# Layer norm's scale and shift on transposed tiles, with a separate path for the residual rows

## Chip, cores, metric

The kernel runs on one core of a Trainium2 chip. The metric is device time in microseconds (us) of one execution, as the median of several runs.

## What is computed

Two layers of a hybrid decoder trunk on a sequence of 1024 tokens with 1024 channels, all in float32. In each layer a mixer (dilated attention, a gated linear recurrence and a state-space branch behind one input projection, joined by one output projection) and a convolutional feed-forward block are each added to the scaled input and normalized:

```python
def _layer_norm(x, g, b):
    xf = x.astype(jnp.float32)
    mu = jnp.mean(xf, axis=-1, keepdims=True)
    var = jnp.mean(jnp.square(xf - mu), axis=-1, keepdims=True)
    y = (xf - mu) * lax.rsqrt(var + LN_EPS) * g.astype(jnp.float32) + b.astype(jnp.float32)
    return y.astype(x.dtype)
...
    for l in range(DEPTH):
...
        h = _layer_norm(DEEPNORM_ALPHA * h + mix, ln1_g[l], ln1_b[l])
        ffn = _conv_ffn(h, w_up[l], ffn_conv_w[l], ffn_conv_b[l], w_down[l])
        h = _layer_norm(DEEPNORM_ALPHA * h + ffn, ln2_g[l], ln2_b[l])
```

So there are four layer norms. Each output h goes two ways: through the next block's projection, and as the residual (times alpha) into the next sum.

## The kernel before

Rows of h are tokens: eight row tiles of 128 tokens x 1024 channels (NT = 8, `ys[0..7]`). A projection needs h with channels along partitions, so each row tile is transposed on TensorE in blocks of 128x128 (`PE.transpose` with `ident`) into a PSUM bank, from which ScalarE copies it. Float32 matmuls are made of three products of a high and a low part: `split(hi, lo, src)` is a ScalarE copy into the rounded type and a VectorE subtraction for the rest.

`layer_norm` (L1274) takes the statistics of a row tile on VectorE (two `bn_stats`, one `bn_aggr`, then a root on ScalarE and a reciprocal on VectorE). It then applies mean, root, scale and shift in one of two ways, chosen per tile by `LN_ON_V` (L40): two `scalar_tensor_tensor` passes of 128x1024 on VectorE, or one ScalarE activation with scale 1/std and bias -mean/std and then a multiply and an add of 128x1024 on VectorE. Along a row scale and shift vary by column, so `ln_params` (L1268) loads them from DRAM broadcast to all 128 partitions (`lg`, `lb`).

The first norm of a layer (names `y`, `ln1`) stands in `after` (L1749), called for each row tile behind the last group of the output projection (`op03...`, `op13...`). The tile is normalized, stored to the DRAM buffer `hres`, and two tiles later given to `M.put` (L1355): eight transposes into two banks (`ht`), four ScalarE copies into `raw` (`hr`). From `raw` it builds, whenever enough columns are there, the seven moving operands of the up-projection (`B11`, `B21`, `B22`, `T1` to `T4`; in the trace `T0...` and `T1...` with the layer ahead). The up-projection `uP` and the down-projection `dP` use a seven-product scheme on 2x2 blocks, so operands are sums and differences of blocks, made on VectorE.

The up-projection goes over 24 pairs of column tiles (`pairs`, L1545). Each pair loads two weight tiles (`wu`), prepares seven weight operands (`wA`, `wS`), issues 84 matmuls, and applies the convolution and the gate (`cg`, `cv`); the product is stored to DRAM (`gd`). Before the down-projection the eight row tiles are loaded back from `hres` as `yf` and scaled by alpha on ScalarE (L1570 to L1574); the down-projection's results are added onto them by VectorE. In layer 0 the second norm (`ln20`, through `lagged`, L1309) stores each tile to `hres` and `to_hT` (L1295) transposes it, with hi taken by ScalarE from PSUM and lo by VectorE from PSUM, for layer 1's input projection (`ups1`, `vps_1`, `q1`, `k1`). Layer 1 loads the rows from `hres` again later as `y` and scales them by alpha (L1732, L1733). The last norm (`ln21`) goes to the output.

Nothing is issued in the order in which it is written. All calls are recorded, and a planner (`Graph`, `make_plan`) gives every call an order and every tile a place: it sweeps the calls forwards and backwards several times with estimated durations, limits how early an instruction may stand before it is due (`AHEAD`), and respects the number of buffers (46 slots of 128x1024, `NSLOT`; 8 half slots; 8 PSUM banks). Each engine then runs its own list strictly in that order; all DMAs are issued from SP's queue. All instructions are issued from one helper, so the trace gives line L146 for all of them, and tiles are told apart by their names.

Of the kernel before, what the change touches and what calls it, by code (L numbers as in the profile page):

```python
# [21 lines left out]
NT = 8  # L22
# [17 lines left out]
LN_ON_V = {"10": (0, 2, 4, 6, 7), "11": (0, 2, 4, 6, 7), "20": (1, 3, 5, 7), "21": (0, 2, 4, 6, 7)}  # L40
# [11 lines left out]
def layout(x, w_in, lru_conv_w, lru_conv_b, lru_wr, lru_br, lru_wi, lru_bi, lru_lambda, s5_a_re, s5_a_im, s5_b_re,  # L52
# [15 lines left out]
    def state4(a):  # L68
# [13 lines left out]
        "fcw": ffn_conv_w.reshape(L, 3, 48, 128).transpose(3, 0, 2, 1), "fcb": chan(ffn_conv_b, 48),  # L82
        "bglu": chan(s5_b_glu, 2), "are": state(s5_a_re), "aim": state(s5_a_im),
# [413 lines left out]
def emit(tc, A, out, planner, trace):  # L497
    nc = tc.nc
    V, ACT, POOL, PE, SP = (Traced(e, planner.calls) for e in (nc.vector, nc.scalar, nc.gpsimd, nc.tensor, nc.sync))
    with ExitStack() as ctx:  # L500
# [48 lines left out]
        def load_w(src, name):  # L549
# [4 lines left out]
            return hi, lo  # L554

# [718 lines left out]
        def layer_norm(i, y, gb, name, by_half=False):  # L1274
# [6 lines left out]
            if by_half:  # L1281
                (a, b), (ga, gg), (ba, bb) = (halves(t) for t in (y, *gb))
                for x, gx, bx in ((a, ga, ba), (b, gg, bb)):
                    stt(x, x, mv[:, 0:1], gx, ALU.subtract, ALU.mult)
                    stt(x, x, mv[:, 2:3], bx, ALU.mult, ALU.add)
            elif i in (LN_ON_V[name[2:4]]):
                stt(y, y, mv[:, 0:1], gb[0], ALU.subtract, ALU.mult)
                stt(y, y, mv[:, 2:3], gb[1], ALU.mult, ALU.add)
            else:
                stt(mv[:, 3:4], mv[:, 0:1], -1.0, mv[:, 2:3], ALU.mult, ALU.mult)  # L1290
                ACT.activation(y, y, AF.Identity, scale=mv[:, 2:3], bias=mv[:, 3:4])
                mul(y, y, gb[0])
                add(y, y, gb[1])

        def to_hT(i, y, name):  # L1295
            if i % 4 == 0:
                hT_tiles(name, i // 4)
            c = slice(i % 4 * 128, i % 4 * 128 + 128)
            for h in range(2):
                ps = bank(f"{name}h{h}")  # L1300
                for k in range(4):
                    PE.transpose(ps[:, k * 128:(k + 1) * 128], y[:, (4 * h + k) * 128:(4 * h + k + 1) * 128], ident)
                for q in range(2):
# [38 lines left out]
        class Moving:  # L1342
# [12 lines left out]
            def put(self, i, y):  # L1355
# [4 lines left out]
                d = slice(i % 4 * 128, i % 4 * 128 + 128)  # L1360
                for h in range(2):
                    ps = bank(f"ht{l}{i}{h}")
                    for k in range(4):
                        PE.transpose(ps[:, k * 128:(k + 1) * 128], y[:, (4 * h + k) * 128:(4 * h + k + 1) * 128], ident)
                    for q in range(2):
                        ACT.activation(t_slice(self.raw[2 * h + q, c], d),
# [419 lines left out]
```

## Time and profile before

| | us |
|---|---|
| median of 3 runs (lowest, highest) | 2337.41 (2333.17, 2340.06) |
| the profiled execution | 2334.8 |
| its span, first to last instruction | 2333.0 |
| TensorE (PE) busy in the span | 2263.2 (97%) |
| VectorE (DVE) busy | 2051.2 (88%) |
| ScalarE (ACT) busy | 1136.1 (49%) |
| DMA, share of 16 engines | 28.0% |

Busy time is the part of the span in which an engine runs an instruction. The granted clock is that of TensorE as a share of full speed. Instructions that follow each other directly on VectorE overlap a little, so from start to start they take less than their busy time.

### The profile page before, as it was taken

The page shows a single profiled execution, that of the slowest core. Times are in us where ns is not written, and L with a number is a line of the kernel's source. Part 1 is how long each engine was busy: PE and PEld are TensorE (multiplying, and loading weights), DVE is VectorE, ACT ScalarE, POOL GpSimd, SP SyncE. Part 2 cuts the span into 40 slices and gives each one's busy share as a digit, 9 for nine tenths or more (in the row PEclk, how much of TensorE's full clock was granted, in tenths as well). Part 3 has the DMA queues.
Part 4 walks back from the last instruction along what each step waited for, and adds up shares of the span by engine and source line. Part 5 has one row for each costly group of instructions (what it writes and reads, how often), then busy time and mean ns, then how long its engine had stood idle before and what let it go on. Part 6 is the DMA issues. An engine that isn't in the chain of part 4 may idle for free.

```text
span 2333.0 us, 28165 instructions
## 1 busy us (share of the span) xinstructions
PE 2263.2 (97%) x10520; PEld 1818.2 (78%) x10520; DVE 2051.2 (88%) x3362; ACT 1136.1 (49%) x1766; POOL 4.0 (0%) x8
## 2 busy tenths in 40 slices
PE   7999999999999999999899999999999999999996
PEld 6877778778888888888678677787888888878885
DVE  8797788998888889999995877789879899899999
ACT  4265673454444446444433646825345454464442
POOL 0000000000000000000000000000000000000000
PEclk9999999989999999999999999999999999999998
DMA  5321141212223226222333211412122232262312
GB/s 195 85 79 44 46 149 55 82 63 94 78 73 101 83 96 225 100 99 100 110 98 92 64 53 42 149 50 100 37 82 82 90 100 99 83 240 80 133 70 90
DMA packets 75257, 221.18 MB, mean 95 GB/s; under 512 B 11696, under 2 KB 20016, under 8 KB 75120
## 3 DMA queue, kind: packets, MB, share of 16 engines
q1 hardware_dynamic: 75120, 219.38, 28.0%
q8 instruction: 82, 1.34, 0.2%
q14 instruction: 55, 0.45, 0.1%
HBM read 163.65 MB, written 48.23 MB: 91 GB/s over the span
## 4 chain that ended last, share of the span: by engine, by line
PE 83%; DVE 13%; ACT 1%; DMA 1%; issue 1%; DVEq 0%; ACTq 0%; SPq 0%
PE uP_n L146 35%; PE dP_n L146 14%; PE o_n L146 3%; DVE yf_n L146 3%; PE s_n L146 2%; PE pt_n L146 2%; PE yps_n L146 1%; DVE daP_n L146 1%; DVE dbP_n L146 1%; DVE cg_n L146 1%; DVE gr_n L146 1%; DMA wu_n<-in_w_up_dram 1%; DVE wr_n L146 1%; DVE cv_n L146 1%; PE ups00c_n L146 1%
## 5 line engine op out<-in xcount | busy, mean ns | idle before, releaser
L146 PE MATMUL dP_n<-dbP_n,daP_n 128*128 128x512 f32 x2016 | 463.3, 392 | 18.3 <-DVE yf_n L146 17.7
L146 PEld LDWEIGHTS dP_n<-dbP_n,daP_n 128*128 128x128 f32 x2016 | 380.5, 189 | 98.9 <-issue 9.5
L146 ACT ACTIVATE dbP_n<-wr_n 128x512 fp32r<-128x512 f32 x168 | 102.0, 627 | 128.8 <-DVE wr_n L146 65.2
L146 DVE SCALAR_TENSOR_TENSOR cg_n<-ga_n,small,cg_n 128x1023 f32<-128x1023 f32 x96 | 122.7, 1280 | 26.6 <-ACT cg_n L146 26.1
L146 ACT ACTIVATE wS_n<-wu_n 128x512 fp32r<-128x512 f32 x144 | 89.9, 629 | 114.9 <-PE uP_n L146 66.7
L146 ACT ACTIVATE wA_n<-wu_n 128x512 fp32r<-128x512 f32 x144 | 88.9, 626 | 95.3 <-PE uP_n L146 47.7
L146 DVE TENSOR_TENSOR yf_n<-yf_n,dP_n 128x512 f32<-128x512 f32 x192 | 127.7, 689 | 3.7 <-PE dP_n L146 2.9
L146 ACT ACTIVATE daP_n<-gr_n 128x512 fp32r<-128x512 f32 x144 | 87.7, 626 | 86.3 <-PE dP_n L146 48.4
L146 DVE SCALAR_TENSOR_TENSOR cv_n<-va_n,small,cv_n 128x1023 f32<-128x1023 f32 x96 | 122.9, 1281 | 6.1 <-ACT cv_n L146 5.3
L146 DVE TENSOR_TENSOR dbP_n<-wr_n,dbP_n 128x512 fp32r<-128x512 f32 x168 | 116.1, 694 | 1.0 <-ACT dbP_n L146 1.0
L146 DVE TENSOR_TENSOR wS_n<-wu_n,wS_n 128x512 fp32r<-128x512 f32 x144 | 98.0, 688 | 15.2 <-ACT wS_n L146 14.8
L146 DVE TENSOR_TENSOR wA_n<-wu_n,wA_n 128x512 fp32r<-128x512 f32 x144 | 97.8, 687 | 7.2 <-ACT wA_n L146 6.9
L146 DVE TENSOR_TENSOR daP_n<-gr_n,daP_n 128x512 fp32r<-128x512 f32 x144 | 99.1, 693 | 1.3 <-ACT daP_n L146 1.2
L146 DVE CUSTOM_DVE_ANT_0 P_n<-s_n,mask_n 128x512 f32<-128x512 f32 (+3 forms) x96 | 55.3, 587 | 45.6 <-PE s_n L146 37.7
L146 ACT ACTIVATE cg_n<-ga_n,small 128x1024 f32<-128x1024 f32 x48 | 59.5, 1242 | 50.8 <-DVE ga_n L146 42.2
L146 ACT ACTIVATE cv_n<-va_n,small 128x1024 f32<-128x1024 f32 x48 | 59.7, 1243 | 42.6 <-DVE va_n L146 26.7
L146 PE MATMUL o_n<-PT_n,vt_n 128*64 128x256 f32 (+1 forms) x480 | 80.2, 380 | 0.0
L146 DVE TENSOR_TENSOR uu_n<-uP_n,p_n 128x512 f32<-128x512 f32 x96 | 65.6, 687 | 14.2 <-PE uP_n L146 14.1
L146 PE MATMUL pt_n<-ident,P_n 128*128 128x128 f32 x432 | 73.7, 281 | 1.2 <-ACT k11r_n L146 0.8
L146 PEld LDWEIGHTS pt_n<-ident,P_n 128*128 128x128 f32 x432 | 50.7, 141 | 28.2 <-issue 16.6
L146 PE MATMUL uP_n<-T0T2h_n,wS_n 128*128 128x512 f32 x192 | 65.3, 401 | 4.1 <-DVE wS_n L146 3.6
L146 PE MATMUL uP_n<-T1T1h_n,wS_n 128*128 128x512 f32 x192 | 63.7, 392 | 3.6 <-ACT T1T1h_n L146 3.6
(2300 smaller groups left out, 5973.7 us busy)
## 6 DMA issues: line engine op xcount, KB each, us to landing
wu_n<-in_w_up_dram SPq DMA_DIRECT2D x96, 512.0 KB, 3.5
gd<-cg_n SPq DMA_DIRECT2D x48, 512.0 KB, 2.8
gr_n<-gd SPq DMA_DIRECT2D x48, 512.0 KB, 4.7
wr_n<-in_w_down_dram SPq DMA_DIRECT2D x48, 512.0 KB, 4.4
hres<-y_n SPq DMA_DIRECT2D x16, 512.0 KB, 2.6
yf_n<-hres SPq DMA_DIRECT2D x16, 512.0 KB, 5.1
xT_n<-in_xT_dram SPq DMA_DIRECT2D x16, 256.0 KB, 5.9
y_n<-in_x_dram SPq DMA_DIRECT2D x8, 512.0 KB, 4.0
```

What stands on the lines that cost most here:

```text
L146: i = f(*args, **kwargs)
```

## The change

Scale and shift leave the row tiles. A row tile is only normalized, always by ScalarE, and stored to `hres` that way. Tiles are transposed two by two: four banks, each with two channel blocks of two tiles; `turned` applies scale and shift while ScalarE evacuates a bank, where they are one number per partition, read from the table of small parameters (`small`, which gets four more entries). `put` and `to_hT` use it; in `to_hT` the evacuation goes to a half slot, and hi and lo are split from there. The residual path applies scale and shift (both multiplied by alpha beforehand) to the rows in a block of its own: it loads a row tile from `hres`, multiplies, adds, and stores it back. For a layer's first norm that block lies in the pairs 12 to 19 of its up-projection (`RES`), one tile to a pair; for the second norm of layer 0 ahead of the second group of attention heads of layer 1 (`RESP`). The scaling by alpha where the rows are loaded is dropped, except for the input x. The last norm is applied by VectorE for all tiles.

```diff
-LN_ON_V = {"10": (0, 2, 4, 6, 7), "11": (0, 2, 4, 6, 7), "20": (1, 3, 5, 7), "21": (0, 2, 4, 6, 7)}
+RES = 12
+RESP = 1
...
+        def normalize(y, name):
+
+            mv = moments(y, name)
+            stt(mv[:, 3:4], mv[:, 0:1], -1.0, mv[:, 2:3], ALU.mult, ALU.mult)
+            ACT.activation(y, y, AF.Identity, scale=mv[:, 2:3], bias=mv[:, 3:4])
+
+        def turned(l, which, ys, i, name, into):
+
+            g, b = par(f"l{which}g", l), par(f"l{which}b", l)
+            for q in range(4):
+                ps = bank(f"{name}{q}")
+                for k in range(2):
+                    for t in range(2):
+                        PE.transpose(ps[:, (2 * k + t) * 128:(2 * k + t + 1) * 128],
+                                     ys[i + t][:, (2 * q + k) * 128:(2 * q + k + 1) * 128], ident)
+                o = into(q)
+                for k in range(2):
+                    ACT.activation(o[:, k, :], ps[:, k * 256:k * 256 + 256], AF.Identity,
+                                   scale=g[:, 2 * q + k:2 * q + k + 1], bias=b[:, 2 * q + k:2 * q + k + 1])
+                yield q, o
+
+        def residual(l, which):
+
+            gb = ln_params(l, which)
+            for t in gb:
+                ACT.activation(t, t, AF.Identity, scale=ALPHA)
+
+            def apply(y):
                 mul(y, y, gb[0])
                 add(y, y, gb[1])
 
-        def to_hT(i, y, name):
+            return apply
...
+        def to_hT(l, ys, i, name):
             if i % 4 == 0:
                 hT_tiles(name, i // 4)
-            c = slice(i % 4 * 128, i % 4 * 128 + 128)
...
-                    ACT.activation(hi, pv, AF.Identity)
-                    sub(lo, pv, hi)
...
+            c = slice(i % 4 * 128, i % 4 * 128 + 256)
+            for q, o in turned(l, 1, ys, i, name, lambda q: two_k(half(f"{name}o{q}"))):
+                split(*(two_k(t)[:, :, c] for t in hT[q, i // 4]), o)
...
-            def put(self, i, y):
+            def put(self, i, ys):
...
+                d = slice(i % 4 * 128, i % 4 * 128 + 256)
+                for _ in turned(l, 0, ys, i, f"ht{l}{i}", lambda q: t_slice(self.raw[q, c], d)):
+                    pass
...
             for n, u in enumerate(pairs[:-2]):
+                if n == RES:
+                    apply = residual(l, 0)
+                if RES <= n < RES + NT:
+                    y = slot(f"yr{l}{n - RES}")
+                    SP.dma_start(out=y, in_=rows(n - RES))
+                    apply(y)
+                    SP.dma_start(out=rows(n - RES), in_=y)
...
-                SP.dma_start(out=y, in_=hres[i * 128:(i + 1) * 128, :])
-                ACT.activation(y, y, AF.Identity, scale=ALPHA)
+                SP.dma_start(out=y, in_=rows(i))
...
+                if l and p == RESP:
+                    apply = residual(l - 1, 1)
+                    for i in range(NT):
+                        y = slot(f"yr{l}{i}")
+                        SP.dma_start(out=y, in_=rows(i))
+                        apply(y)
+                        SP.dma_start(out=rows(i), in_=y)
...
             def after(i):
-                layer_norm(i, ys[i], gb, f"ln1{l}{i}")
-                SP.dma_start(out=hres[i * 128:(i + 1) * 128, :], in_=ys[i])
-                if i >= 2:
-                    M.put(i - 2, ys[i - 2])
+                normalize(ys[i], f"ln1{l}{i}")
+                SP.dma_start(out=rows(i), in_=ys[i])
+                if i in (3, 5, 7):
+                    M.put(i - 3, ys)
...
                 if n == 0:
-                    M.put(6, ys[6])
-                if n == 1:
-                    M.put(7, ys[7])
+                    M.put(6, ys)
```

## Rows read from the trace of the kernel before

**Rows 1.** The page: span, busy time by engine, chain that ended last by engine.
```profile
span 2333.0 us, 28165 instructions
PE 2263.2 (97%) x10520; PEld 1818.2 (78%) x10520; DVE 2051.2 (88%) x3362; ACT 1136.1 (49%) x1766; POOL 4.0 (0%) x8
...
PE 83%; DVE 13%; ACT 1%; DMA 1%; issue 1%; DVEq 0%; ACTq 0%; SPq 0%
```

**Rows 2.** Table by stage: stretch and length, busy us by engine, granted clock, DMA.
```profile
440.00:500.00 60.00, 52.66 (x224) 40.85 (x223) 59.21 (x87) 38.24 (x68) 0.00 (x0) 0.89 0.19 64
...
550.00:890.00 340.00, 340.00 (x1500) 281.31 (x1499) 285.59 (x376) 153.67 (x211) 1.91 (x2) 1.00 0.26 87
890.00:1100.00 210.00, 209.94 (x926) 173.51 (x926) 207.31 (x333) 106.07 (x172) 0.00 (x0) 1.00 0.39 138
1100.00:1200.00 100.00, 86.16 (x403) 70.56 (x402) 99.64 (x184) 41.49 (x80) 0.00 (x0) 0.93 0.32 107
...
1310.00:1590.00 280.00, 280.00 (x1404) 213.51 (x1403) 221.54 (x379) 150.56 (x236) 0.00 (x0) 1.00 0.21 68
1590.00:1660.00 70.00, 64.17 (x293) 49.81 (x292) 68.38 (x107) 39.07 (x81) 0.00 (x0) 0.93 0.24 86
...
1700.00:2050.00 350.00, 349.81 (x1538) 288.19 (x1537) 309.44 (x404) 168.12 (x228) 0.00 (x0) 1.00 0.29 96
```

**Rows 3.** TensorE's waits: for whom, us in total, times, longest.
```profile
PE dP_n L146 <- DVE yf_n L146: 17.7, 4, 8.4
...
PE uP_n L146 <- ACT T1T1h_n L146: 3.6, 1, 3.6
```

**Rows 4.** Timeline of VectorE, 425 to 500 us: start, busy us, instruction.
```profile
424.32 1.22 DVE L146 TENSOR_TENSOR y_n<-y_n,lb_n 128x1024 f32<-128x1024 f32 x1
425.46 1.28 DVE L146 SCALAR_TENSOR_TENSOR y_n<-y_n,mv__ln,lb_n 128x1024 f32<-128x1024 f32 x1
...
456.61 1.28 DVE L146 SCALAR_TENSOR_TENSOR y_n<-y_n,mv__ln,lb_n 128x1024 f32<-128x1024 f32 x1
...
477.95 1.23 DVE L146 TENSOR_TENSOR T0T4l_n<-hr_n,T0T4h_n 128x1024 fp32r<-128x1024 f32 x1
```

**Rows 5.** Timeline of TensorE, same stretch; in brackets idle before and releaser.
```profile
466.32 0.72 PE L146 MATMUL uP_n<-T0T1h_n,wS_n 128*128 128x512 f32 x1 [2.16 <-ACT T0T1h_n L146]
468.07 0.79 PE L146 MATMUL uP_n<-T0T1l_n,wS_n 128*128 128x512 f32 x1 [1.02 <-DVE T0T1l_n L146]
469.33 0.79 PE L146 MATMUL uP_n<-T0T2h_n,wS_n 128*128 128x512 f32 x1 [0.47 <-ACT T0T2h_n L146]
...
475.22 1.22 PE L146 MATMUL uP_n<-T0T2h_n,wS_n 128*128 128x512 f32 x2 [3.65 <-DVE wS_n L146]
```

**Rows 6.** Timeline of VectorE, then of TensorE, 1100 to 1182 us.
```profile
1128.37 1.28 DVE L146 SCALAR_TENSOR_TENSOR yf_n<-yf_n,mv__ln,lg_n 128x1024 f32<-128x1024 f32 x1
...
1174.59 1.29 DVE L146 SCALAR_TENSOR_TENSOR yf_n<-yf_n,mv__ln,lb_n 128x1024 f32<-128x1024 f32 x1
...
1149.53 7.09 PE L146 MATMUL dP_n<-dbP_n,daP_n 128*128 128x512 f32 x24 [8.41 <-DVE yf_n L146]
```

**Rows 7.** Timeline of VectorE, 1590 to 1660 us.
```profile
1595.44 1.27 DVE L146 SCALAR_TENSOR_TENSOR y_n<-y_n,mv__ln,lg_n 128x1024 f32<-128x1024 f32 x1
...
1619.37 1.28 DVE L146 SCALAR_TENSOR_TENSOR y_n<-y_n,mv__ln,lb_n 128x1024 f32<-128x1024 f32 x1
```

**Rows 8.** ScalarE's groups by tile and shape: count, busy us, mean ns, idle before.
```profile
L146 ACT ACTIVATE y_n<-y_n 128x1024 f32<-128x1024 f32 x16 | 16.8, 1053 | 10.3 <-DMA y_n<-hres 5.0 <-PE o_n L146 3.2 <-DMA y_n<-in_x_dram 2.0
L146 ACT ACTIVATE y_n<-y_n,mv__ln 128x1024 f32<-128x1024 f32 x6 | 7.6, 1263 | 2.2 <-DVE mv__ln L146 2.2
```

**Rows 9.** Weight split's group on ScalarE; DMA issues: count, KB, us to landing.
```profile
L146 ACT ACTIVATE wA_n<-wu_n 128x512 fp32r<-128x512 f32 x144 | 88.9, 626 | 95.3 <-PE uP_n L146 47.7 <-DMA wu_n<-in_w_up_dram 14.0 <-DVE cv_n L146 7.7
...
wu_n<-in_w_up_dram SPq DMA_DIRECT2D x96, 512.0 KB, 3.5
gd<-cg_n SPq DMA_DIRECT2D x48, 512.0 KB, 2.8
```

More of the change, by code (lines that the diff above doesn't have):

```diff
@@ L554, in load_w, with rows @@
             return hi, lo
+        def rows(i):
+            return hres[i * 128:(i + 1) * 128, :]
         def half(name):
@@ L1280, in layer_norm @@
             rstd(mv[:, 2:3], mv[:, 1:2], 1, 1)
[L1281 to L1291, printed above, removed]
+            return mv
@@ new lines, in layer_norm @@
+        def layer_norm(y, gb, name, by_half=False):
+            mv = moments(y, name)
+            for a, ga, ba in zip(*(halves(t) for t in (y, *gb))) if by_half else ((y, *gb),):
+                stt(a, a, mv[:, 0:1], ga, ALU.subtract, ALU.mult)
+                stt(a, a, mv[:, 2:3], ba, ALU.mult, ALU.add)
+        def normalize(y, name):
+            mv = moments(y, name)
+            stt(mv[:, 3:4], mv[:, 0:1], -1.0, mv[:, 2:3], ALU.mult, ALU.mult)
+            ACT.activation(y, y, AF.Identity, scale=mv[:, 2:3], bias=mv[:, 3:4])
@@ L1359, in put @@
                         self.raw[q, c] = slot(f"hr{l}{q}{c}")
[L1360 to L1366, printed above, removed]
-                                       ps[:, q * 256:q * 256 + 256].rearrange("p (k c) -> p k c", k=2), AF.Identity)
-                if i == 3:
+                d = slice(i % 4 * 128, i % 4 * 128 + 256)
+                for _ in turned(l, 0, ys, i, f"ht{l}{i}", lambda q: t_slice(self.raw[q, c], d)):
+                    pass
+                if i == 2:
                     for name, q0 in (("B11", 0), ("B21", 2)):
@@ L1597, in store @@
                         def store(i):
-                            SP.dma_start(out=hres[i * 128:(i + 1) * 128, :], in_=ys[i])
-                        after, tail = lagged(ys, gb, f"ln2{l}", store)
+                            SP.dma_start(out=rows(i), in_=ys[i])
+                        after, tail = lagged(l, ys, f"ln2{l}", store)
                 def product(p, ops, i):
@@ L1731, in emit @@
                 y = slot(f"y{l}{i}")
-                SP.dma_start(out=y, in_=(A["x"] if l == 0 else hres)[i * 128:(i + 1) * 128, :])
-                ACT.activation(y, y, AF.Identity, scale=ALPHA)
+                SP.dma_start(out=y, in_=A["x"][i * 128:(i + 1) * 128, :] if l == 0 else rows(i))
+                if l == 0:
+                    ACT.activation(y, y, AF.Identity, scale=ALPHA)
                 ys.append(y)
@@ L1749, in after @@
             def after(i):
-                layer_norm(i, ys[i], gb, f"ln1{l}{i}")
-                SP.dma_start(out=hres[i * 128:(i + 1) * 128, :], in_=ys[i])
-                if i >= 2:
-                    M.put(i - 2, ys[i - 2])
+                normalize(ys[i], f"ln1{l}{i}")
+                SP.dma_start(out=rows(i), in_=ys[i])
+                if i in (3, 5, 7):
+                    M.put(i - 3, ys)
             out_group(l, sp, 3, rl, ys, after)
```

40 lines of the change are left out of this document (17 added, 23 removed).

## The prediction

> **What bounds the kernel now.** I read the page first. TensorE is busy for 97% of the span and the chain that ended last lies on it for 83%, with 13% on VectorE [rows 1]. So little is to be had outside the 69.8 us in which TensorE is idle (2333.0 less 2263.2), and what VectorE costs matters only where TensorE waits for it. Next I read the table by stage, to see where those 69.8 us lie [rows 2]. Three stretches are the seams where a layer norm stands between two matmul stages: 440 to 500 us (first norm of layer 0, seam A) has 7.34 us idle, 1100 to 1200 (second norm of layer 0, seam B) 13.84, 1590 to 1660 (first norm of layer 1, seam C) 5.83. That is 27.0 us. In each VectorE is busy nearly throughout (59.21 of 60, 99.64 of 100, 68.38 of 70). Elsewhere TensorE is full: 340.00 of 340, 280.00 of 280, 349.81 of 350 us. The list of TensorE's waits says the same from the other side: what it waits for is a tile that VectorE, or ScalarE right behind VectorE, writes last [rows 3].
>
> The same table holds a second loss. The mean granted clock of the seams is 0.89, 0.93 and 0.93, and 1.00 elsewhere [rows 2]. Two levels occur, 2.4 and 1.2 GHz, so 13.2, 14.0 and 9.8 us were spent at the lower one (for A 60 x 0.11 / 0.5). In A the fall comes with the gaps that end at 466.32 and 475.22 us [rows 5]. A part of the slow time is idle and already counted; of what is busy, half is lost. In A the gaps of 1.02, 0.47 and 3.65 us lie in it [rows 5], so about 8 us are busy and 4 are lost; for B I take 3 and for C 3.4. Together the seams cost 11.3 + 16.8 + 9.2 = 37.3 us. No gain can be much more.
>
> **What leaves VectorE at the seams.** Each norm today ends in two passes of 128x1024 on VectorE, either two scalar_tensor_tensor (1.28 us busy each) or, behind ScalarE's normalization, a multiply and an add (1.22 each, the next one starting 1.14 us on) [rows 4]. Afterwards there is none: ScalarE does (y - mean) x rstd for every tile, and scale and shift ride on the evacuation of the transposes, where they lie along partitions. What counts is what leaves the stretch in which VectorE is saturated. In A, 12 such passes lie from 424.32 to 456.61, and VectorE then works without a break until the last operand of the up-projection at 477.95 [rows 4]. At about 1.17 us from start to start these are 14.0 us, against 11.3 of loss. In B there are 16 passes between 1128.37 and 1174.59, 18.7 us against 16.8, and the largest gap, 8.41 us, ends at 1149.53 with seven of the 16 before it [rows 6]. In C there are ten from 1595.44 to 1619.37, 11.7 us against 9.2 [rows 7]. So in each seam the credit just exceeds the loss.
>
> **What joins the seams.** ScalarE gets the normalization of the tiles that had none: five tiles more in A and in C, four more in B, at 1.263 us each [rows 8]. Every evacuation now takes a scale and a bias per partition. Nearest row: the same Identity on 128x1024 takes 1.263 us with both and 1.053 without [rows 8], so 0.21 us more on each of 32 evacuations, 6.7 us a seam. In B each operand of the next layer also passes one more ScalarE copy (16 of 128x512, 0.63 us each by the weight split's row [rows 9]). ScalarE's sum goes from 38.2 to about 51 of 60 us in A and from 41.5 to about 63 of 100 in B [rows 2]: no bound, but a hop on the chain of the last pair. Transposes are as many as before; tiles go two by two, so an even tile waits for its odd neighbour, which the operands built from column pairs did before too. I take back 1 us in A, 2.5 in B (eight evacuations 0.21 longer, and the copy) and 1.5 in C, where the margin is thinnest. The reach of these terms is 0 to half of each seam's loss. What is left to gain is 10.3 + 14.3 + 7.7 = 32.3 us.
>
> One rule of the Trainium skill speaks against the move: its page "ScalarE: Activation LUTs", section "Rules for kernel authors", says that adds and multiplies belong on VectorE and not on ScalarE. The rows show for this type and size 1.22 us a pass on VectorE and 1.263 for scale and shift together on ScalarE [rows 4, 8], so here the trace does not bear it out; by the rule, ScalarE would be the later engine and rival 3 would hold.
>
> **What moves into other stages.** The residual needs the scaled rows too. A block per row tile loads it, multiplies, adds and stores it again: 8 tiles, three times. Two of these blocks lie in pairs 12 to 19 of the up-projections, one tile to a pair, the third ahead of the second attention group of layer 1. Each tile is two VectorE passes, 2.3 us from start to start; 18.4 us a block, 55 us in all, which roughly equals what the seams lose. The cover: in 550 to 890 us TensorE issues 1500 matmuls in 340 us, so a pair of 84 lasts 19.0 us; VectorE is busy for 285.59 of 340, which leaves 3.0 us a pair. In layer 1 it is 309.44 of 350, or 2.2 us a pair for 2.3 of work [rows 2]: just full. That VectorE is full need not stop TensorE: from 890 to 1100 us VectorE is busy for 207.31 of 210 and TensorE for 209.94 [rows 2]. The attention stage has 58 us free [rows 2]. Bounds: 0 (all covered, or a little below, since VectorE's busy time shrinks when instructions stand back to back) to 18.4 us for each block. I take 1.5 for each of the two in the up-projections, nearest to the row of 890 to 1100, and nothing in attention.
>
> Each tile also adds a load and a store on SP's queue (48 of 512 KB in all; the loads of scales and shifts stay eight, six of them now ahead of a block instead of a seam). SP waits before each store until VectorE has added; the next weight load stands behind it. The store of each pair's gated product (gd) waits for VectorE in the same way 48 times already, and it takes no TensorE time. A weight load lands 3.5 us after its issue [rows 9]. ScalarE loses 24 scalings by alpha (1.05 us each by their twin's row [rows 8]) and gains six on the parameters: nothing, as it has room.
>
> The order of all instructions is written by a planner that starts anew with other calls. Stages that are gapless now may get small gaps, or lose the few they have. Bounds: -3 to +10 us; I take 3.
>
> **Sum.** The profiled execution took 2334.8 us, 1.8 around its span. 2334.8 - 32.3 + 3 + 3 = 2308.5. The median of the runs is 2.6 us above the profiled one, so I forecast 2311 us, a gain of 1.1%.
>
> **Rivals.** Rival 1, slower: room in SBUF. The seven operands of the up-projection hold 28 of 46 slots (7 names, 2 halves, hi and lo); 18 are left for a pair's 14 tiles and the loads of the next. The residual holds two parameters and one or two row tiles through eight pairs a layer. If the next pair's weights then come only when a slot falls free, TensorE waits up to the 3.5 us of landing in each of 16 pairs: 56 us. 2311 + 56 - 3 = 2364; from 2.4 us a pair it is slower than before by over 0.3%. Against it: no weight load is among TensorE's waits [rows 3], and ScalarE waits for them 14.0 us over 144 copies [rows 9]. The skill's page "Trainium Kernel Development and Optimization", section "Best Practices", says that regular bubbles can mean that SBUF ran out; the trace has none there. Rival 2, no change: the planner pushes the residual towards the down-projection, where VectorE is full, or up-projection and attention take most of it: 30 to 40 of the 55 us show, 2311 + 32 - 3 = 2340, from about 2330. Rival 3, a half gain: ScalarE's longer evacuations become the last link at the seams. 2311 + 16 = 2327.
>
> **How the numbers follow.** Forecast (2297 to 2320) 0.64; rival 3 and smaller leaks (2320 to 2330) 0.17; rival 2 0.09; rival 1 0.10. Of 2337, 0.3% is 7 us, about the least that a measurement of this kernel tells from no change. Faster by more: 0.64 + 0.17 = 0.81; within: 0.09; slower: 0.10. The range takes in the ceiling, 2337.4 - 37.3 less a few us by which a new order may be luckier, and reaches up into rival 2: 2297 to 2335.
>
> **What would show it.** Right: in the stretches of the three seams TensorE's idle falls from 27 us to under 8 and the granted clock to 0.97 or more; VectorE's sum over the span stays within 10 us; the waits for yf in seam B are gone; the up-projections hold over 99% on TensorE with VectorE some 18 us busier. Wrong: TensorE waits for weight loads in pairs 12 to 19 (rival 1), VectorE multiplies and adds of rows after the down-projection has begun (rival 2), gaps at the seams that end on ScalarE's evacuations (rival 3).

## Result and profile after

| | us |
|---|---|
| before, median of 4 runs (lowest, highest) | 2336.65 (2333.17, 2340.06) |
| after, median of 4 runs (lowest, highest) | 2303.27 (2301.57, 2303.53) |
| ratio, with its 95% interval | 0.9856 [0.9839, 0.9873] |
| profiled execution of after, its span | 2303.5, 2301.7 |

The kernel became 1.4% faster; the forecast was 2311 us, 1.1%. The page of after answers to [rows 1]: span, busy time by engine, the chain that ended last by engine, then the new DMA issues (count, KB, us to landing). Instructions that stood at L146 before stand at L149 now.

```profile
span 2301.7 us, 28256 instructions
...
PE 2242.8 (97%) x10520; PEld 1811.4 (79%) x10520; DVE 2045.1 (89%) x3357; ACT 1154.0 (50%) x1773; POOL 4.0 (0%) x8
...
PE 84%; DVE 10%; ACT 3%; DMA 2%; issue 1%; DVEq 0%; ACTq 0%; SPq 0%
...
yr_n<-hres SPq DMA_DIRECT2D x24, 512.0 KB, 3.8
hres<-yr_n SPq DMA_DIRECT2D x24, 512.0 KB, 3.2
```

VectorE's sum hardly moved (2051.2 to 2045.1 us) while its share of the chain fell from 13% to 10%: the passes were not saved, they were moved to where TensorE doesn't wait for them.

Since the two orders differ, equal clock times don't hold equal work. From here on the span is cut at five matmuls that every version has: the first of the last group of layer 0's output projection (`op03`), the last of its up-projection (`uP`), the last of the first product of layer 1's input projection (`ups1`), and for layer 1 again the first of the last output group (`op13`) and the last of the up-projection. This gives six stages: mixer of layer 0 (all up to that last output group); A (last output group, first norm, up-projection); B (down-projection, second norm, first product of layer 1); mixer of layer 1 (the rest of the input projection, attention, the other output groups); C, as A for layer 1; the end. The table by stage, first of before, then of after; columns: stretch and length, busy us (and count) of PE, PEld, DVE, ACT, POOL, granted clock, DMA share, GB/s.

```profile
0.00:406.90 406.90, 391.05 (x1996) 302.80 (x1997) 334.06 (x739) 216.32 (x336) 2.04 (x6) 0.99 0.30 94
406.90:918.50 511.60, 503.91 (x2226) 413.58 (x2225) 451.34 (x618) 240.84 (x357) 1.91 (x2) 0.99 0.28 94
918.50:1194.60 276.10, 262.26 (x1172) 216.19 (x1172) 273.12 (x466) 127.20 (x224) 0.00 (x0) 0.98 0.32 114
1194.60:1569.80 375.20, 370.34 (x1900) 283.00 (x1899) 291.34 (x518) 200.61 (x310) 0.00 (x0) 0.99 0.25 75
1569.80:2081.00 511.20, 504.10 (x2226) 412.31 (x2225) 456.25 (x623) 244.41 (x362) 0.00 (x0) 0.99 0.28 96
2081.00:2333.00 252.00, 231.54 (x1009) 190.35 (x1007) 245.11 (x403) 106.72 (x180) 0.00 (x0) 0.97 0.28 103
```

```profile
0.00:397.50 397.50, 383.68 (x1992) 298.71 (x1993) 331.52 (x739) 214.71 (x336) 2.04 (x6) 0.99 0.31 95
397.50:901.10 503.60, 500.71 (x2230) 411.83 (x2229) 451.03 (x622) 254.86 (x366) 1.92 (x2) 1.00 0.32 111
901.10:1163.20 262.10, 260.19 (x1181) 214.35 (x1180) 258.43 (x442) 138.02 (x233) 0.00 (x0) 1.00 0.34 119
1163.20:1544.50 381.30, 365.45 (x1882) 283.27 (x1881) 305.14 (x535) 192.78 (x303) 0.00 (x0) 0.97 0.31 99
1544.50:2048.60 504.10, 501.64 (x2234) 412.65 (x2233) 453.31 (x624) 256.58 (x370) 0.00 (x0) 1.00 0.31 108
2048.60:2301.70 253.10, 231.09 (x1008) 190.61 (x1006) 245.69 (x400) 97.04 (x167) 0.00 (x0) 0.96 0.33 117
```

The stages that hold the seams became 8.0, 14.0 and 7.1 us shorter, 29.1 together; TensorE's idle time in them fell from 28.6 us (7.7 + 13.8 + 7.1) to 7.3 (2.9 + 1.9 + 2.5), and the granted clock rose from 0.99, 0.98 and 0.99 to 1.00. Two other stages moved that no step of the sum had priced: the mixer of layer 0, which the change does not touch, is 9.4 shorter, and the mixer of layer 1 is 6.1 longer, with 15.9 us idle and a clock of 0.97. The end is 1.1 longer. In all -31.3 us.

TensorE's waits in after, answering to [rows 3]: for whom, us in total, times, longest.

```profile
PE dP_n L149 <- DVE yf_n L149: 11.8, 2, 10.9
PE pt_n L149 <- DVE P_n L149: 10.1, 5, 4.9
...
PE uP_n L149 <- DVE uu_n L149: 5.0, 7, 2.0
```

The wait of 10.9 us for yf stands at the end of the kernel; of those in seam B, 8.41 the longest before [rows 6], one of 0.8 us is left. New is the second line: attention's transposes wait for the probabilities `P`. ScalarE's groups (count, busy us, mean ns, idle before): the evacuations of before, then evacuations and normalizations of after, answering to [rows 8]:

```profile
L146 ACT ACTIVATE hr_n<-ht_n 128x256 f32<-128x256 f32 x64 | 21.4, 389 | 11.8 <-PE ht_n L146 11.5
...
L149 ACT ACTIVATE hr_n<-ht_n,small 128x256 f32<-128x256 f32 x64 | 32.7, 574 | 6.0 <-PE ht_n L149 5.9
...
L149 ACT ACTIVATE y_n<-y_n,mv__ln 128x1024 f32<-128x1024 f32 x16 | 20.0, 1250 | 3.8 <-DVE mv__ln L149 3.8
```

VectorE's last operand of the first up-projection, answering to the last line of [rows 4], and the table for the stretch from the start of A to the end of that operand, first of before, then of after:

```profile
461.98 1.22 DVE L149 TENSOR_TENSOR T0T4l_n<-hr_n,T0T4h_n 128x1024 fp32r<-128x1024 f32 x1
```

```profile
406.90:479.20 72.30, 64.95 (x296) 51.31 (x295) 69.63 (x108) 35.32 (x74) 0.00 (x0) 0.91 0.20 75
...
397.50:463.20 65.70, 64.34 (x313) 52.64 (x311) 56.96 (x102) 47.41 (x83) 0.00 (x0) 1.00 0.21 81
```

### The profile page after: what moved, and what is told of

It is laid out like the page before. It is cut to its first block, busy times and chain, and to the rows that moved or that the text cites. A ratio compares the mean times of both kernels' runs of the same rounds, so it can differ in the third digit from the quotient of the medians.

```text
span 2301.7 us, 28256 instructions
## 1 busy us (share of the span) xinstructions
PE 2242.8 (97%) x10520; PEld 1811.4 (79%) x10520; DVE 2045.1 (89%) x3357; ACT 1154.0 (50%) x1773; POOL 4.0 (0%) x8
## 4 chain that ended last, share of the span: by engine, by line
PE 84%; DVE 10%; ACT 3%; DMA 2%; issue 1%; DVEq 0%; ACTq 0%; SPq 0%
PE uP_n L149 34%; PE dP_n L149 17%; PE o_n L149 3%; PE s_n L149 2%; PE pt_n L149 2%; DVE yf_n L149 1%; PE yps_n L149 1%; DVE cg_n L149 1%; DMA wu_n<-in_w_up_dram 1%; DVE daP_n L149 1%; PE ups00c_n L149 1%; DVE dbP_n L149 1%; PE gtps01c_n L149 1%; PE vps_01c_n L149 1%; DVE cv_n L149 1%
## 5 line engine op out<-in xcount | busy, mean ns | idle before, releaser
L149 PE MATMUL dP_n<-dbP_n,daP_n 128*128 128x512 f32 x2016 | 462.2, 391 | 12.6 <-DVE yf_n L149 11.8
L149 PEld LDWEIGHTS dP_n<-dbP_n,daP_n 128*128 128x128 f32 x2016 | 379.6, 189 | 92.5 <-issue 12.5
L149 ACT ACTIVATE dbP_n<-wr_n 128x512 fp32r<-128x512 f32 x168 | 102.8, 627 | 104.7 <-DVE wr_n L149 49.7
L149 ACT ACTIVATE wA_n<-wu_n 128x512 fp32r<-128x512 f32 x144 | 89.9, 628 | 122.4 <-PE uP_n L149 41.9
L149 ACT ACTIVATE wS_n<-wu_n 128x512 fp32r<-128x512 f32 x144 | 90.2, 630 | 111.5 <-DVE wu_n L149 41.3
L149 ACT ACTIVATE daP_n<-gr_n 128x512 fp32r<-128x512 f32 x144 | 89.5, 628 | 112.8 <-PE dP_n L149 48.2
L149 DVE SCALAR_TENSOR_TENSOR cg_n<-ga_n,small,cg_n 128x1023 f32<-128x1023 f32 x96 | 122.9, 1280 | 23.4 <-ACT cg_n L149 22.6
L149 DVE SCALAR_TENSOR_TENSOR cv_n<-va_n,small,cv_n 128x1023 f32<-128x1023 f32 x96 | 122.8, 1280 | 16.2 <-ACT cv_n L149 16.0
L149 DVE TENSOR_TENSOR yf_n<-yf_n,dP_n 128x512 f32<-128x512 f32 x192 | 127.9, 689 | 4.4 <-PE dP_n L149 2.4
L149 DVE TENSOR_TENSOR dbP_n<-wr_n,dbP_n 128x512 fp32r<-128x512 f32 x168 | 116.0, 694 | 0.3 <-ACT dbP_n L149 0.3
L149 DVE TENSOR_TENSOR daP_n<-gr_n,daP_n 128x512 fp32r<-128x512 f32 x144 | 99.8, 694 | 2.4 <-ACT daP_n L149 2.4
L149 DVE TENSOR_TENSOR wS_n<-wu_n,wS_n 128x512 fp32r<-128x512 f32 x144 | 98.2, 687 | 3.3 <-ACT wS_n L149 2.8
L149 DVE TENSOR_TENSOR wA_n<-wu_n,wA_n 128x512 fp32r<-128x512 f32 x144 | 97.8, 687 | 3.1 <-ACT wA_n L149 2.9
L149 ACT ACTIVATE cg_n<-ga_n,small 128x1024 f32<-128x1024 f32 x48 | 59.7, 1243 | 73.9 <-DVE ga_n L149 51.2
L149 PE MATMUL pt_n<-ident,P_n 128*128 128x128 f32 x432 | 74.3, 285 | 11.2 <-DVE P_n L149 10.1
L149 PEld LDWEIGHTS pt_n<-ident,P_n 128*128 128x128 f32 x432 | 53.4, 144 | 33.7 <-DVE P_n L149 11.6
L149 DVE CUSTOM_DVE_ANT_0 P_n<-s_n,mask_n 128x512 f32<-128x512 f32 (+3 forms) x96 | 55.4, 586 | 22.6 <-PE s_n L149 21.9
L149 ACT ACTIVATE cv_n<-va_n,small 128x1024 f32<-128x1024 f32 x48 | 59.4, 1238 | 24.7 <-DVE va_n L149 18.5
L149 PE MATMUL o_n<-PT_n,vt_n 128*64 128x256 f32 (+1 forms) x480 | 71.1, 375 | 0.0
L149 DVE TENSOR_TENSOR uu_n<-uP_n,p_n 128x512 f32<-128x512 f32 x96 | 65.9, 687 | 3.7 <-PE uP_n L149 3.4
L149 PE MATMUL uP_n<-T1T4h_n,wA_n 128*128 128x512 f32 x192 | 64.0, 394 | 2.1 <-DVE uu_n L149 2.1
L149 PE MATMUL uP_n<-T0T3h_n,wS_n 128*128 128x512 f32 x192 | 63.4, 391 | 2.3 <-DVE uu_n L149 2.3
## 6 DMA issues: line engine op xcount, KB each, us to landing
wu_n<-in_w_up_dram SPq DMA_DIRECT2D x96, 512.0 KB, 3.5
gd<-cg_n SPq DMA_DIRECT2D x48, 512.0 KB, 2.9
gr_n<-gd SPq DMA_DIRECT2D x48, 512.0 KB, 4.4
wr_n<-in_w_down_dram SPq DMA_DIRECT2D x48, 512.0 KB, 5.1
yr_n<-hres SPq DMA_DIRECT2D x24, 512.0 KB, 3.8
hres<-yr_n SPq DMA_DIRECT2D x24, 512.0 KB, 3.2
hres<-y_n SPq DMA_DIRECT2D x16, 512.0 KB, 2.6
yf_n<-hres SPq DMA_DIRECT2D x16, 512.0 KB, 5.2
```

The source lines that it names most:

```text
L149: i = f(*args, **kwargs)
```

## Experiments

Stage lengths in us of the profiled executions, in brackets TensorE's idle time, and the median of the runs with its ratio to before (timed anew beside each):

| version | mixer 0 | A | B | mixer 1 | C | median, ratio |
|---|---|---|---|---|---|---|
| before | 406.9 | 511.6 (7.7) | 276.1 (13.8) | 375.2 (4.9) | 511.2 (7.1) | 2336.65 |
| after | 397.5 | 503.6 (2.9) | 262.1 (1.9) | 381.3 (15.9) | 504.1 (2.5) | 2303.27, 0.9856 |
| first norms only | 400.6 | 501.5 (0.5) | 279.9 (14.3) | 362.2 (2.2) | 505.2 (3.3) | 2304.22, 0.9854 [0.9839, 0.9869] |
| second norm only | 404.0 | 520.7 (16.3) | 264.3 (4.1) | 381.3 (10.3) | 513.3 (8.7) | 2337.13, 1.0003 [0.9993, 1.0012] |
| no residual blocks | 398.7 | 505.1 (2.5) | 262.9 (2.3) | 355.0 (0.0) | 501.9 (1.2) | 2280.42, 0.9754 [0.9740, 0.9769] |
| later block | 399.7 | 508.0 (5.7) | 263.0 (2.7) | 362.3 (2.3) | 502.8 (2.6) | 2290.44, 0.9800 [0.9785, 0.9815] |
| passes back | 415.9 | 516.8 (8.9) | 278.0 (11.4) | 373.9 (7.1) | 512.8 (9.5) | 2349.55, 1.0044 [1.0027, 1.0060] |
| before, other order 1 | 426.0 | 512.5 (8.9) | 285.6 (20.3) | 362.8 (1.2) | 512.0 (8.9) | 2347.02, 1.0035 [1.0019, 1.0051] |
| before, other order 2 | 413.8 | 512.9 (9.1) | 277.4 (14.6) | 367.3 (4.5) | 511.0 (7.4) | 2337.78, 0.9998 [0.9988, 1.0009] |
| after, other order 1 | 407.2 | 504.9 (3.9) | 260.7 (2.0) | 374.1 (12.5) | 501.8 (0.4) | 2305.31, 0.9875 [0.9853, 0.9897] |
| after, other order 2 | 404.3 | 504.1 (3.4) | 261.3 (1.5) | 383.6 (12.5) | 502.0 (1.3) | 2307.91, 0.9881 [0.9865, 0.9897] |
| later block, other order 1 | 413.8 | 504.5 (4.1) | 261.1 (1.2) | 368.2 (0.0) | 500.6 (1.1) | 2292.95, 0.9813 [0.9794, 0.9831] |
| residual on GpSimd | 401.1 | 544.0 (29.3) | 262.3 (3.1) | 376.6 (8.8) | 532.7 (26.0) | 2374.33, 1.0152 [1.0137, 1.0167] |
| residual in place | 397.5 | 505.1 (4.1) | 260.6 (1.7) | 363.8 (0.3) | 502.1 (2.1) | 2281.86, 0.9768 [0.9753, 0.9784] |

**One norm at a time.** Layer 0's second norm goes back to the passes on VectorE and to transposes tile by tile, and its residual block goes:

```diff
-                normalize(ys[i], f"{name}{i}")
+                old_norm(i, ys[i], gb, f"{name}{i}")
...
-                if l and p == RESP:
-                    apply = residual(l - 1, 1)
...
```

> Only the first norm of each layer is changed (seams A and C, and the residual block in pairs 12 to 19); the second norm of layer 0 stays as before, with scale and shift on the rows. Theory (the seams pay, each by the VectorE passes that leave it): from the start of the last output group to the end of the up-projection layer 0 gets 8 us shorter and layer 1 7 us, seam B keeps its 14 us of idle, and outside nothing moves by plan but a few us either way by the new order: 15 us less than before, 2321 (2313 to 2329). Rival (the gain is mostly a lucky order of the whole program): the gain does not follow the seams; seam B shrinks as well, or A and C do not.

And the other way round, the two first norms as before, without the blocks in the up-projections:

```diff
-                normalize(ys[i], f"ln1{l}{i}")
+                old_norm(i, ys[i], gb, f"ln1{l}{i}")
...
-                if n == RES:
-                    apply = residual(l, 0)
...
```

> Only the second norm of layer 0 is changed (seam B, and its residual block ahead of the second attention group of layer 1); the first norms stay as before. Theory: the down-projection of layer 0 and the first product of layer 1 together get 14 us shorter, seams A and C keep 7.3 and 5.8 us of idle; if the residual block is what costs attention of layer 1 some 8 us, that stage is 8 us longer here too and the whole is 2331; if that was only the order, 2323. Rival (lucky order): gains appear at A and C too, or not at B.

The changed seams became shorter and the others didn't. The stages of "first norms only", A, B and C as above:

```profile
400.60:902.10 501.50, 501.02 (x2230) 411.35 (x2229) 454.07 (x626) 257.19 (x369) 0.00 (x0) 1.00 0.32 111
902.10:1182.00 279.90, 265.56 (x1173) 218.47 (x1173) 275.52 (x469) 119.83 (x212) 1.91 (x2) 0.97 0.33 116
...
1544.20:2049.40 505.20, 501.90 (x2234) 412.49 (x2233) 455.14 (x627) 254.31 (x368) 0.00 (x0) 1.00 0.33 110
```

A and C are 10.1 and 6.0 us shorter than before; B keeps its 14.3 us idle. In "second norm only" B is 11.8 shorter, C 2.1 longer. But the whole times came out wrong: 33 us gained with the first norms alone, nothing with the second. 2321 had been expected of the first, 2323 or 2331 of the second. Stages outside the changed seams moved: the mixer of layer 1 by -13.0 us in the first, stage A by +9.1 in the second, where TensorE waits 14.35 us at one point for a weight operand (`wS`). So the order of the work is drawn anew each time, and a whole time says little about a part. The changed stages by themselves gained 27.9 us (10.1, 6.0 and 11.8), near the 29.1 with both; but with the unchanged ones, which became longer, A + B + C fell by only 12.3 us in the first and 0.6 in the second. So these two runs show that a changed seam gains, not exactly how much.

**The passes alone.** The rival to the passes is that taking tiles two by two, or the longer evacuation, made the difference. This version keeps all of the change and puts two passes back behind ScalarE's normalization:

```diff
             ACT.activation(y, y, AF.Identity, scale=mv[:, 2:3], bias=mv[:, 3:4])
+            for _ in range(2):
+                stt(y, y, 0.0, y, ALU.mult, ALU.add)
```

> The changed kernel with two VectorE passes of 128x1024 put back behind each normalization at the three seams (y times 0 plus y, 1.28 us each like the scale and shift that left); all else stays, the pairing, the scale and shift on the evacuation, the residual blocks. Theory (the seams were bound by VectorE and these passes were the cost): the seams lose what they gained, 8 + 14 + 7 = 29 us and a little more for the work that now stands twice, 2332 (2325 to 2345), with VectorE saturated again and TensorE waiting for operands written by VectorE. Rival (the gain came from pairing the tiles or from leaving PSUM reads to ScalarE): under 2312.

Its table by stage (A, B, C), and TensorE's waits at its seams:

```profile
415.90:932.70 516.80, 507.91 (x2226) 415.43 (x2225) 465.41 (x634) 254.16 (x365) 0.96 (x1) 0.99 0.31 106
932.70:1210.70 278.00, 266.62 (x1184) 218.59 (x1184) 273.02 (x453) 139.22 (x236) 0.96 (x1) 0.98 0.33 116
...
1584.60:2097.40 512.80, 503.31 (x2230) 414.02 (x2229) 469.70 (x638) 255.04 (x369) 0.00 (x0) 0.99 0.31 105
```

```profile
PE ln20t_n L149 <- DVE mv__ln L149: 5.1, 1, 5.1
PE uP_n L149 <- ACT T1T1h_n L149: 4.7, 1, 4.7
```

A + B + C is 1307.6 us against 1269.8 in after and 1298.9 in before; idle 29.8 us against 7.3. The median is 46 us above after and 5 above the range that had been expected; of the profiled execution's excess 37.8 us lie in A, B and C, and 18.4 in the mixer of layer 0, at a clock of 0.96, which no seam explains (the mixer of layer 1 is 7.4 shorter). The loss at the seams comes back with the passes, so they are its cause; pairing and evacuation alone do not make the gain. VectorE is again nearly full at B (67.92 of 70 us, 1130 to 1200) and at C (48.88 of 50, 1610 to 1660), but has only 35.11 of 40 at A (460 to 500). There the passes also lengthen each tile's way to its transposes, and the runs don't separate that from VectorE's load.

**No residual.** Both blocks go, the one in the up-projections (it runs in both layers) and the one in attention.

```diff
-                if n == RES:
-                    apply = residual(l, 0)
...
-                if l and p == RESP:
-                    apply = residual(l - 1, 1)
...
```

> The changed kernel without its three residual blocks: the rows that are added later lack scale, shift and alpha, so that part of the computation is left out. It prices the 55 us of VectorE work and 48 transfers that moved. Theory (covered by VectorE's free time in the up-projections): layer 0 and 1 up-projections at most 3 us shorter together; attention of layer 1 up to 8 us shorter if the block is to blame there: 2293 to 2302. Rival (the moved work is not covered): 2270 or less.

Stages A, mixer of layer 1, and C:

```profile
398.70:903.80 505.10, 502.62 (x2232) 411.96 (x2231) 434.11 (x604) 252.53 (x365) 1.91 (x2) 1.00 0.26 90
...
1166.70:1521.70 355.00, 355.00 (x1887) 277.35 (x1887) 286.29 (x506) 185.51 (x296) 0.00 (x0) 1.00 0.26 79
1521.70:2023.60 501.90, 500.73 (x2230) 411.90 (x2229) 438.81 (x613) 253.71 (x368) 0.00 (x0) 1.00 0.27 89
```

In the two up-projections the blocks add 16.9 and 14.5 us of work to VectorE (451.03 less 434.11, 453.31 less 438.81) and, A and C together, 0.7 us to the time (1007.7 against 1007.0). They are covered: A + C takes 1005.1 to 1010.8 us in the seven versions and orders that keep both blocks on VectorE without passes put back, so 0.7 is less than an order is worth. The 23 us by which this version beats after (2293 to 2302 had been expected) lie in the mixer of layer 1: 355.0 against 381.3.

**The block in attention, elsewhere.** The same block ahead of the third instead of the second group of heads:

```diff
-RESP = 1
+RESP = 2
```

> The residual block of layer 1's attention stands one group of heads later (RESP 2 instead of 1), nothing else. Theory (the block holds up the first softmax tiles, where TensorE now idles 15.6 us between the first scores and the output projection of layer 1): that idle falls to about 5 and the whole by 8 to 10 us, 2294. Rival (that idle is the planner's order of the first scores, whatever stands beside): 2300 to 2306 with the same idle.

The mixer of layer 1 then is

```profile
1170.70:1533.00 362.30, 360.00 (x1889) 279.28 (x1888) 303.64 (x525) 191.59 (x303) 0.00 (x0) 1.00 0.32 103
```

with nearly all of VectorE's added work in it (303.64 us; after 305.14, without blocks 286.29), and the median 13 us below after. So most of the cost is not the work but its place. What it does at the first place, the chain of waits of after shows (start, us, what):

```profile
1274.29 0.93 ACT P_n L149 x2
1275.24 0.16 DVE nb__1041_1850 L149
1275.41 1.12 DVE yr_n L149
1276.53 0.47 DVE P_n L149
1276.99 0.08 DVE nb__1050_1856 L149
1277.08 1.12 DVE yr_n L149
1278.20 1.13 DVE P_n L149 x2
...
1280.89 1.14 DVE yr_n L149
```

Here VectorE is itself the chain: softmax's products and reciprocals, rotations of q and k, and between them three passes of the residual, 3.4 us that show one for one. TensorE's gaps behind them in the timeline are 1.46, 0.76 and 2.50 us; but the largest, 4.93, ends at 1265.12, before the first pass of the block. These gaps go with the slow clock; the line of the largest, and the table of after in stretches of 20 us:

```profile
1265.12 0.69 PE L149 MATMUL pt_n<-ident,P_n 128*128 128x128 f32 x2 [4.93 <-DVE P_n L149]
```

```profile
1260.00:1280.00 20.00, 13.51 (x56) 10.98 (x55) 18.03 (x36) 12.21 (x18) 0.00 (x0) 0.66 0.51 159
1280.00:1300.00 20.00, 15.28 (x64) 10.74 (x63) 18.38 (x35) 7.03 (x11) 0.00 (x0) 0.83 0.22 79
```

So by this chain and these gaps the three passes account for some 3 to 5 us, an estimate. The rest must come from the order in which the planner set everything around them; by which link, the runs don't settle.

**Other orders of the same work.** To see how much an order is worth by itself, a constant of the planner is changed, in before, in after and in the version with the later block; the instructions stay the same.

```diff
-HANDOVER = {"PE": 230, "DVE": 90, "ACT": 120, "POOL": 100, "SP": 0}
+HANDOVER = {"PE": 230, "DVE": 100, "ACT": 120, "POOL": 100, "SP": 0}
```

> The kernel before with one estimate of the planner changed (a VectorE result counts as seen by another engine after 100 instead of 90 ns), no work changed: it shows how far the time moves by a new order alone. Theory: the three seams keep their 25 to 30 us of idle, attention stages move by several us, the whole stays in 2325 to 2350. Rival (a new order alone gives what the change gave): 2310 or less.

> The changed kernel with the planner's estimate of VectorE's handover at 100 instead of 90 ns, no work changed. If the block ahead of the second attention group costs by its place, the stretch from the end of layer 1's first product to its last output group stays at 375 to 385 us (381 in both runs that have the block there so far). If that was the order of these two runs, it falls to 355 to 370 and the whole to about 2285 to 2290. The seams stay at 270 us less 1000, that is at 1265 to 1275 us together in either case.

> The later block (RESP 2) in a new order (VectorE's handover at 100 ns). If the place decides, attention of layer 1 stays at 355 to 367 us and the whole at 2283 to 2297; if the first run with the later block was a lucky order, 370 to 382 us there and 2300 or more.

```diff
-AHEAD, AHEAD_BACK = (5000, 10000), (10000, 20000)
+AHEAD, AHEAD_BACK = (5500, 10500), (10000, 20000)
```

> The kernel before with another planner setting (an instruction may stand 5.5 or, for SP, 10.5 us ahead of its due time instead of 5 and 10): a second new order of the same work. Theory: 2325 to 2350 with the seams' idle kept. Rival: 2310 or less.

> The changed kernel with the planner's limit on running ahead at 5.5 and 10.5 us instead of 5 and 10, no work changed: a second new order, with the same two outcomes for attention of layer 1 as the run beside it (375 to 385 us by place, 355 to 370 by order).

Three orders of before take 2337 to 2347 us, three of after 2303 to 2308: the change is worth 29 to 44 us between any two of these orders. It is the seams that separate them: A + B + C is 1298.9, 1310.1 and 1301.3 us in before, and 1269.8, 1267.4 and 1267.4 in after. The mixer of layer 0, which no version edits, spreads from 397.5 to 426.0 us. Not all of that is order: TensorE is idle there for 13.6 to 26.5 us and spends 0 to 44.4 us at the lower clock level, most in the longest, and less the idle time and half of the busy time at that level (an estimate of what the clock costs) every version has 381 to 387 us. The longest (before, other order 1) is also the profile of an execution of 2356.0 us, where the other four took 2340.6 to 2351.0. With the block ahead of the second head group (after, its two other orders, second norm only, passes back) the mixer of layer 1 takes 373.9 to 383.6, 378.8 on average; with the block later or in place 362.3, 368.2 and 363.8, 364.8 on average. Against the other places the block's first one costs about 14 us, between 6 (374.1 against 368.2, the same constant) and 19 (381.3 against 362.3). Lengths alone don't settle it, since versions with no block there take 355.0 to 375.2, and the 368.2 holds 24 us at the lower clock level in an execution that ran 9 us longer than the others (see the end). TensorE's idle time tells more: 7.1 to 15.9 us with the block on VectorE at the first place, 0.0 to 2.3 with it later or in place, 0.0 to 4.9 with none. Two stages came out 1 us outside what had been expected, 374.1 (375 to 385) and 368.2 (355 to 367).

**Residual on GpSimd.** GpSimd is free (4.0 us busy), so multiply and add could go there:

```diff
-                mul(y, y, gb[0])
-                add(y, y, gb[1])
+                POOL.tensor_tensor(y, y, gb[0], op=ALU.mult)
+                POOL.tensor_tensor(y, y, gb[1], op=ALU.add)
```

with `RESP = 2`.

> The residual's multiplies and adds go to GpSimd, which is idle, with the block of layer 1 at its later place (RESP 2): VectorE loses the 55 us that had moved. Theory (what the residual still costs is VectorE's time): between the run without residual (2280) and the one with the later block (2290), 2284. Rival (the cost is transfers and buffers, or GpSimd and VectorE hinder each other): 2290 or more, with longer VectorE instructions beside GpSimd's.

It is the slowest of all: 84 us above the later block, 66 of them in A and C (36.0 and 29.9). Why is told below, under the hardware.

**Residual in place.** If place is what costs in attention, the second norm's scale and shift can wait until layer 1 loads the rows anyway, which also saves the block's eight loads and stores:

```diff
-                if l and p == RESP:
-                    apply = residual(l - 1, 1)
...
+            if l:
+                apply = residual(l - 1, 1)
...
                 if l == 0:
                     ACT.activation(y, y, AF.Identity, scale=ALPHA)
+                else:
+                    apply(y)
```

> The block of layer 1's attention is gone: scale and shift are applied where layer 1 loads its rows for the residual sum anyway, so 8 loads and 8 stores of 512 KB and their buffers fall away, the 18.4 us of VectorE work stay, later. Theory (place and traffic decide, VectorE has room before the output projection): attention of layer 1 as without residual or a little above, 355 to 363 us, the whole 2281 to 2292. Rival (VectorE's passes are what costs wherever they stand): attention and the output groups 375 us or more, 2300.

```profile
1163.20:1527.00 363.80, 363.49 (x1897) 278.46 (x1896) 304.88 (x530) 188.71 (x299) 0.00 (x0) 1.00 0.25 77
```

2281.86 us, 2.3% below before and 21 us below after; TensorE has 0.3 us idle where after had 15.9, at an unchanged load of VectorE (304.88 against 305.14 us). This version beats both kernels, and comes within 1 to 3 us of the one without any residual block (ratios 0.9768 and 0.9754).

## Why the prediction was right

**The bound and the seams: right, seam by seam.** Less the 1.5 us that the residual was to cost in A and in C, the forecast was 8.8, 14.3 and 6.2 us, 29.3 together; the stages gave 8.0, 14.0 and 7.1, 29.1 together. The step "what leaves the stretch in which VectorE is saturated" held: up to the last operand of the up-projection VectorE was busy for 69.63 of 72.3 us in A and is for 56.96 of 65.7 now, 12.7 us less where 14.0 were forecast. That operand (T4's low part, start 461.98) is begun 64.5 us into stage A, before it was 71.1 (477.95 less 406.9, [rows 4]); VectorE has 8.7 us free on the way there, before it had 2.7. That the passes and not the pairing do it, the version with the passes put back shows. The three signs named for the seams came out, over the longer stages A, B and C: 7.3 us idle (under 8 forecast), clock 1.00 (0.97), the waits for yf in seam B gone but for 0.8 us. The clock's term held too: by the clock's records TensorE was busy for 8.5, 6.4 and 6.7 us at the lower level in A, B and C of before, half of which is 4.3, 3.2 and 3.4 us (4, 3 and 3.4 forecast), and for none in after. That the division among the seams fits to under 1 us each is partly luck, since each of the three stages moves by 2 to 4 us among the orders of after and of the later block.

**What joins the seams: right, a little too dear.** The evacuation takes 574 ns against 389 before, 185 more and not 210; the normalization 1.250 us against 1.263 [rows 8]. Rival 3 falls: in A, B and C the only gap that ends on an evacuation by ScalarE is 0.27 us, in B; the longest gap left is 2.02 us, in A, for sums of the up-projection's results (`uu`) on VectorE. The rule that the prediction weighed, from the Trainium skill's page "ScalarE: Activation LUTs", section "Rules for kernel authors", would have had these adds and multiplies stay on VectorE; here the trace doesn't bear it out, since ScalarE had room and VectorE was what the seams waited for.

**Residual in the up-projections: right, and over-priced.** 0.7 us for both in place of 3 (the version without blocks), less than A + C differs by order. That VectorE nearly full need not stop TensorE was the row that decided [rows 2], and TensorE holds 99.4% of A and 99.5% of C. Rival 1 (slots) falls with it: in A and C TensorE waits for `uu` and `ga` alone, for no weight operand. So does rival 2 for the up-projections: the passes run at 685 to 800 and 1833 to 1937 us, inside them. What is left of rival 2 is attention.

**Residual in attention: wrong.** The step "nothing in attention", since 58 us of VectorE are free there, is the term that was mis-sized. Against before, which has no block there, the stage is 6.1, 11.3 and 16.3 us longer in the three orders; against the version without blocks it is 26.3 longer, above the 18.4 us that had been written down as the upper bound. The share of free time was read over the whole stage; but ahead of the second head group VectorE is the chain itself (18.03 and 18.38 of 20 us busy), and since VectorE runs its list in order, the softmax behind a row pass waits for it (1.12 to 1.14 us each in the chain above). That accounts for 3 to 5 us; how the rest comes about stays open.

**The planner's order: wrong in sign and size.** +3 us were taken, with -3 as the lower bound; outside the seams and the mixer of layer 1 the time moved by -8.3 (-9.4 in the mixer of layer 0, +1.1 at the end). 397.5 to 426.0 us in a stage that no version edits shows that the bounds were too narrow, and that clock and idle time there were left out of them. Whether the change has a part in the -9.4 is open: the nine versions with the change in the first norms and without passes put back take 397.5 to 413.8, the three of before 406.9 to 426.0.

**Sum.** The seams were right, and of the rest attention (+6.1 against 0), the residual in the up-projections, which is in the seams' sum, and the order (-8.3 against +3) partly offset: -31.3 us on the spans against the -26.3 forecast. The time lies inside the range, for reasons of which two were not those given; that these two errors partly cancel is luck.

## To carry to other kernels

Count passes by the stretch in which they stand: 38 row passes in the saturated stretches of three seams were worth 29 us, and 32 passes spread over two matmul stages cost 0.7, less than an order is worth, although they nearly filled VectorE there. Free time of an engine over a whole stage is no cover for work that is put in the middle of a dependent chain on that engine; cut the stage into pieces of some 20 us and look at the chain of waits where the work would stand. Where a planner sets the order, time two or three orders of both kernels, and look at idle time and granted clock as well as length, before any difference of a stage is put down to the edit.

## What the hardware showed

**VectorE's passes with two inputs in SBUF are held up beside GpSimd.** GpSimd's pass of 128x1024 takes 2785 ns where VectorE's takes 1220 (groups of the version on GpSimd, then of after: count, busy us, mean ns).

```profile
L149 POOL TENSOR_TENSOR yr_n<-yr_n,lg_n 128x1024 f32<-128x1024 f32 x24 | 66.8, 2785 | 1300.7 <-DMA yr_n<-hres 755.5 <-ACT lg_n L149 537.5 <-DVE cg_n L149 7.6
```

```profile
L149 DVE SCALAR_TENSOR_TENSOR cv_n<-va_n,small,cv_n 128x1023 f32<-128x1023 f32 x96 | 122.8, 1280 | 16.2 <-ACT cv_n L149 16.0
...
L149 DVE TENSOR_TENSOR yr_n<-yr_n,lg_n 128x1024 f32<-128x1024 f32 x24 | 29.2, 1220 | 2.0 <-DMA yr_n<-hres 2.0
```

That alone need not cost time, since GpSimd is busy with these passes for some 135 us of 2369.5. But VectorE's convolution, two passes with two inputs in SBUF, takes 6.44 us beside it and not 2 x 1.28. The timelines of GpSimd, VectorE and TensorE of that version (start, busy us, in brackets idle before and releaser):

```profile
789.54 2.91 POOL L149 TENSOR_TENSOR yr_n<-yr_n,lg_n 128x1024 f32<-128x1024 f32 x1 [5.36 <-DMA yr_n<-hres]
792.53 3.20 POOL L149 TENSOR_TENSOR yr_n<-yr_n,lb_n 128x1024 f32<-128x1024 f32 x1
...
790.37 6.44 DVE L149 SCALAR_TENSOR_TENSOR cv_n<-va_n,small,cv_n 128x1023 f32<-128x1023 f32 x2 [0.18 <-ACT cv_n L149]
...
799.80 0.79 PE L149 MATMUL uP_n<-T0T3h_n,wS_n 128*128 128x512 f32 x1 [6.76 <-DVE uu_n L149]
```

TensorE then waits 6.76 us for `uu`, queued behind on VectorE; in A it idles for 29.3 us and in C for 26.0. The Trainium skill's page "SBUF — State Buffer", section "Who interferes with whom", says that a VectorE instruction with two SBUF inputs contends with a GpSimd instruction that reads SBUF, that the shared ports are an exclusive lock, and that the order of issue decides who is blocked. The trace agrees: VectorE's two passes take 3.16 and 3.24 us, and each ends 1.08 us behind one of GpSimd's (793.53 behind 792.45, 796.81 behind 795.73), so a part of each ran only once GpSimd's pass was done. Not every instruction is held up: `uu`, with one of its inputs in PSUM, takes 0.68 us also where it overlaps a pass of GpSimd (4 of 96).

**The clock falls without a gap.** In the later block's other order TensorE's clock falls in the mixer of layer 1 although its records show no idle time there (368.2 of 368.2 us busy): granted 0.76 and 0.64 in these two stretches, so that 9.6 and 14.4 of 20 us ran at 1.2 GHz. The clock falls at 1230.4 us; from 1226.9 on TensorE issues the short matmuls `yps` back to back, and the last gap before lies 62 us back (0.30 us, ending at 1168.58). That profiled execution was the longest of the four (2302.9 us; the others 2291 to 2294).

```profile
1220.00:1240.00 20.00, 20.00 (x89) 15.17 (x87) 10.66 (x10) 8.24 (x9) 0.00 (x0) 0.76 0.25 68
1240.00:1260.00 20.00, 20.00 (x72) 15.97 (x72) 7.46 (x10) 7.14 (x8) 0.00 (x0) 0.64 0.31 98
```

What brought the clock down there, no run shows.
